# Making a weight tile's low part in two GpSimd instructions of half the width

## The chip, the cores and the metric

The kernel runs on one core of a Trainium2 chip. The metric is the device time of one execution in microseconds; the time before is the median of three runs. All that is read from inside an execution comes from one profiled run of the kernel.

## What is computed

One layer of a decoder trunk on 2048 positions of width 1024, all in float32:

```python
h = rmsnorm(x, norm_mix_w) * (1.0 + sc1) + sh1
proj = h @ w_in                      # 1024 x 3624
o_a = hgrn2_mixer(...)               # gated linear recurrence, 4 heads, chunkwise
o_b = dsa_mixer(...)                 # indexer, top 256 keys of each query, softmax over them
o_c = conv_module(...)               # GLU, causal depthwise conv (31 taps), LayerNorm, swish
x = x + g1 * (concat([o_a, o_b, o_c]) @ w_out)
h = rmsnorm(x, norm_mlp_w) * (1.0 + sc2) + sh2
x = x + g2 * (square(relu(h @ mlp_w1)) @ mlp_w2)      # 1024 -> 4096 -> 1024
return rmsnorm(x, final_norm_w)
```

The six vectors `sh1` ... `g2` come from `silu(c) @ ada_w + ada_b`.

## The kernel before

**Matrix products in three parts.** TensorE's fast float32 form drops low bits, so each operand is split into a high part (a copy rounded to that form) and a low part (the rest: source minus high part), and a product is three: high x high, high x low of the activation, low of the weight x high. The low part of the weight is used last of the three. A weight tile is 128 partitions x 1024 elements: 8 pieces of 128x128 or 4 of 128x256 (`mm_T`, L350; `n_part`, L1158).

**How a weight tile comes about.** `fetch_w` loads it into `wraw` (two buffers) by a DMA that SyncE issues; `split_w` takes a `whi` and a `wlo` (two buffers each) and calls `split`, where ScalarE casts the high part (L256) and GpSimd subtracts (L257). `split` has other callers, with tiles of 128x512 in two dimensions: the hidden activations of the MLP (`hl`) and the mixers' outputs (`ml`). `next_w` keeps one split tile and up to two loads ahead of the product that runs. The raw buffer is free for the next load when its low part is made, and SyncE's queue issues all loads in order.

**The stages.** The positions go in four blocks of 512. Block 0 of the input projection loads and splits `w_in`, and `keep_w` writes both parts to DRAM; blocks 1 to 3 load them ready made (tile `wk`), with no split. Beside it run the recurrence (`hgrn_gen`), the convolution (`conv_gen`), the indexer (`index_gen`), the key search (`topk_gen`) and attention (`attn_gen`) as generators that are stepped between products. Then come the output projection and the MLP, block by block; here every block loads and splits its weights anew, and the rest of indexer, search and attention runs beside it. Before the last block, `tsum_gen` adds quarters of MLP weights on VectorE and writes the sums to DRAM (`tsr`).

**The last block.** It goes through the MLP by a Strassen scheme: `produce` makes split tiles named X, Y, Z and W for each unit. X and Z are tiles of `swh`/`swl` (128 x 2 x 512), Y is `swy`, W is `sww` (a 128x512 tile in two dimensions). The string `LO_W` ("GVVG", or "GVGG" for odd units below 24) says which engine makes the low part (L1485): X and W are GpSimd's, Y is VectorE's, Z is VectorE's or, in the odd units, GpSimd's. The sums on activations (`s_parts`, L1359 to L1366) run on both engines. A product there uses one half of X, Y or Z, and the next product the other half.

**What sets the order.** The program is written as tiles and operations with a priority; when it is built, a planner walks it with a model of times, puts each engine's instructions in one fixed order, and sets the waits. On the chip each engine works through its order.

Of the kernel before, what the change touches and what calls it, by code (L numbers as in the profile page):

```python
# [8 lines left out]
F32 = mybir.dt.float32  # L9
# [7 lines left out]
OP = mybir.AluOpType  # L17
# [60 lines left out]
def trunk(ctx, tc, x, c, ada_w, ada_b, norm_mix_w, norm_mlp_w, w_in, hg_lb_logits,  # L78
# [3 lines left out]
    V, A, G, T = nc.vector, nc.scalar, nc.gpsimd, nc.tensor  # L82
# [18 lines left out]
    def nm(s):  # L101
        uid[0] += 1
        return f"{s}_{uid[0]}"
# [148 lines left out]
        rpow(rs, ss, 1, 1.0 / n)  # L252
        return rs

    def split(src, hi, lo, lo_eng=None):
        A.copy(hi, src)  # L256
        (lo_eng or G).tensor_tensor(lo, src, hi.bitcast(F32), OP.subtract)  # L257

    def to_act_steps(xh, acol, bcol, ah, al, mid=None):
        for k in range(NK):  # L260
# [37 lines left out]
    def split_w(raw, kk, m):  # L298
        hi = wp.tile([P, kk, m], F32R, tag="whi", bufs=WH, name=nm("whi"))
        lo = wp.tile([P, kk, m], F32R, tag="wlo", bufs=WL, name=nm("wlo"))  # L300
        split(raw, hi, lo)
        return hi, lo
# [812 lines left out]
    for pieces, ev, _ in in_units:  # L1115
        if ev in (ev_hi, ev_sv):
            o0, n, src = pieces[0]
# [52 lines left out]
    def mix_tiles(b, kh):  # L1170
        hh, hl = [], []
        for k in range(4):
            hi = mp.tile([P, TB], F32R, tag="hh", bufs=HB, name=nm("mh"))
            lo = mp.tile([P, TB], F32R, tag="hl", bufs=HB, name=nm("ml"))
            r = mp.tile([P, TB], F32, tag="hr", bufs=MR, name=nm("mr"))
            dma(r, mx_d[b][kh * 4 + k])
            split(r, hi, lo)
            hh.append(hi)
            hl.append(lo)
        return hh, hl  # L1180
# [141 lines left out]
    def eng(pat, i):  # L1322
        return G if pat[i] == "G" else V
# [94 lines left out]
    def strassen_prepare():  # L1418
# [4 lines left out]
        def fetch(u):  # L1423
            if u >= len(units) or u in raws:
                return
            what, g, i = units[u]
            r1 = wp.tile([P, 2, TB], F32, tag="wraw", bufs=WR, name=nm("wr1"))
            r2 = sx.tile([P, 4, TB], F32, tag="wr2", bufs=2, name=nm("wr2"))
            if u < NTS:
                quarter_dma(r1[:, 0], u, 0, 0)  # L1430
                dma(r1[:, 1], ts_d[u][:, 1])
                quarter_dma(r2[:, 2], u, 1, 1)
                dma(r2[:, 3], ts_d[u][:, 3])
                quarter_dma(r2[:, 0], u, 1, 0)
                dma(r2[:, 1], ts_d[u][:, 2])
            else:
                for dst, kh, nh in ((r1[:, 0], 0, 0), (r1[:, 1], 0, 1), (r2[:, 0], 1, 0), (r2[:, 2], 1, 1)):
                    quarter_dma(dst, u, kh, nh)
            raws[u] = r1, r2
# [3 lines left out]
        def t_sums(u):  # L1443
            r1, r2 = raws[u]
            t1 = xp.tile([P, TB], F32, tag="tf", bufs=2, name=nm("t1"))
            b11, b12, b21, t4, b22, t2 = r1[:, 0], r1[:, 1], r2[:, 0], r2[:, 1], r2[:, 2], r2[:, 3]
            pat = T_W if units[u][0] == "m1" else T_W2
            if u < NTS:
                dma(t1, ts_d[u][:, 0])
            else:  # L1450
                eng(pat, 0).tensor_tensor(t1, b12, b11, OP.subtract)
                eng(pat, 1).tensor_tensor(t2, b22, t1, OP.subtract)
                eng(pat, 2).tensor_tensor(b12, b22, b12, OP.subtract)
                eng(pat, 3).tensor_tensor(t4, b21, t2, OP.subtract)
            srcs[u] = {"X": r1, "Y": r2[:, 2:], "Z": r2[:, :2], "W": t1}
# [6 lines left out]
        def produce():  # L1462
            if not stream:
                return
            u, which = stream.pop(0)
            if which == "X" and u not in summed:
                fetch(u)
                t_sums(u)
                summed.add(u)
            if which == TSW and u + 1 < len(units):  # L1470
                fetch(u + 1)
                t_sums(u + 1)
                summed.add(u + 1)
            src = srcs[u][which]
            if which in "XZ":
                hi = wp.tile([P, 2, TB], F32R, tag="whi", bufs=WH, name=nm("swh"))
                lo = wp.tile([P, 2, TB], F32R, tag="wlo", bufs=WL, name=nm("swl"))
            elif which == "Y":
                hi, lo = [xp.tile([P, 2, TB], F32R, tag="xt", bufs=4, name=nm("swy")) for _ in range(2)]
            else:  # L1480
                hl = xp.tile([P, 2, TB], F32R, tag="xt", bufs=4, name=nm("sww"))
                hi, lo = hl[:, 0], hl[:, 1]
            A.copy(hi, src)
            lo_w = "GVGG" if u < NTS and u % 2 else LO_W
            eng(lo_w, "XYZW".index(which)).tensor_tensor(lo, src, hi.bitcast(F32), OP.subtract)  # L1485
            if which == "W":
                hi, lo = hl[:, 0:1], hl[:, 1:2]
            split_[u, which] = hi, lo
            if which == FEW:
                fetch(u + 2)  # L1490
# [3 lines left out]
        def early_start():  # L1494
            fetch(0)
            t_sums(0)
            summed.add(0)

        st3.update(units=units, produce=produce, split=split_, early=early_start)

    def strassen_block(b):
# [223 lines left out]
```

## Time and profile before

| | |
|---|---|
| median of 3 runs | 3166.78 us (3162.09 to 3168.3) |
| the profiled execution | 3161.17 us, of which the span of its instructions is 3159.5 us |
| granted TensorE clock, mean | 0.956 |
| busy: PE, DVE, ACT, POOL | 2859.4, 2085.6, 1537.0, 1715.5 us |
| weight tiles' low parts on GpSimd, 128x1024 | 257 of `wlo` (635.5 us), 42 of `swl` (109.5 us) |

PE is TensorE's matmuls, PEld its weight loads, DVE is VectorE, ACT ScalarE, POOL GpSimd, SP SyncE. Times of day within the span count from its first instruction. An engine's busy time includes time in which an instruction has started and is held up.

### The profile page before, as it was taken

The numbers are of one execution on the slowest core, as the hardware profiler recorded it, in microseconds if no ns is written. First come the engines' busy times: TensorE is split into PE (matmuls) and PEld (weight loads), VectorE is DVE, ScalarE is ACT, GpSimd is POOL, SyncE is SP. The second block draws the span as 40 slices with busy tenths as digits, with TensorE's granted clock in tenths as the row PEclk, the third lists the DMA queues.
The fourth block names the chain that finished last, engine by engine and source line by source line (L and its number), as shares of the span: only waits on it lengthen the run. The fifth ranks groups of instructions, "written<-read, shape, count | busy, mean of one in ns | idle before, by whom it ended". The sixth has DMA issues, their size and how long they took to land.

```text
span 3159.5 us, 50407 instructions
## 1 busy us (share of the span) xinstructions
PE 2859.4 (91%) x18352; PEld 2573.1 (81%) x18352; DVE 2085.6 (66%) x3673; ACT 1537.0 (49%) x2879; POOL 1715.5 (54%) x1231
## 2 busy tenths in 40 slices
PE   5979988898999989999999999998898898889987
PEld 4767868777787879888888889898787888889987
DVE  7785486867436444847776757576979631477787
ACT  3435444445313244555556556455544444456653
POOL 6555162225205255555767566576665656756675
PEclk9989999998999999999999999999999999999998
DMA  7856665564655343434546444455799953455533
GB/s 261 267 175 235 221 191 188 192 214 162 196 195 165 119 151 97 136 118 121 157 140 207 138 124 149 122 163 160 241 284 300 299 184 121 143 192 171 175 113 104
DMA packets 479413, 560.08 MB, mean 177 GB/s; under 512 B 32615, under 2 KB 371884, under 8 KB 479148
## 3 DMA queue, kind: packets, MB, share of 16 engines
q1 hardware_dynamic: 478992, 556.65, 55.9%
q8 instruction: 145, 2.38, 0.3%
q14 instruction: 120, 0.98, 0.1%
q10 hardware_dynamic: 156, 0.07, 0.0%
HBM read 458.30 MB, written 98.31 MB: 176 GB/s over the span
## 4 chain that ended last, share of the span: by engine, by line
PE 54%; DVE 22%; DMA 9%; issue 6%; ACT 4%; POOL 3%; SPq 1%; DVEq 0%; POOLq 0%; ACTq 0%
PE mm L350 18%; PE ax L1158 17%; PE mm L1158 5%; DVE cacc L523 2%; DMA adw<-in_ada_w_dram 2%; DVE s L752 2%; DVE cum L850 2%; DMA tsr<-in_mlp_w_dram 2%; PE po L932 1%; PE ix L745 1%; PE at L920 1%; SPq L106 1%; PE ax L632 1%; PE at L898 1%; DMA wr<-ts_d 1%
## 5 line engine op out<-in xcount | busy, mean ns | idle before, releaser
L257 POOL TENSOR_TENSOR wlo<-wraw,whi 128x1024 fp32r<-128x1024 f32 x257 | 635.5, 2473 | 479.6 <-ACT whi L256 343.0
L256 ACT CAST whi<-wraw 128x1024 fp32r<-128x1024 f32 x257 | 270.0, 1050 | 346.7 <-PE ax L1158 127.7
L752 DVE SCALAR_TENSOR_TENSOR s<-r,iw_s,s 128x512 f32<-128x512 f32 (+3 forms) x266 | 301.9, 1135 | 199.8 <-ACT r L747 197.1
L1158 PE MATMUL ax<-whi,hh 128*128 128x256 f32 x1600 | 282.9, 291 | 43.9 <-DVE acc L1302 32.8
L350 PE MATMUL mm<-ah,wk 128*128 128x512 f32 x1104 | 300.9, 405 | 8.1 <-issue 2.5
L1158 PE MATMUL ax<-whi,hl 128*128 128x256 f32 x1600 | 280.2, 289 | 2.2 <-POOL hl L257 2.2
L1158 PEld LDWEIGHTS ax<-whi,hh 128*128 128x128 f32 x1600 | 237.5, 195 | 54.4 <-DVE acc L1302 33.9
L350 PE MATMUL mm<-ah,whi 128*128 128x512 f32 x936 | 263.2, 406 | 16.3 <-DVE slo L463 9.3
L1158 PE MATMUL ax<-wlo,hh 128*128 128x256 f32 x1600 | 275.1, 287 | 0.0
L930 POOL TENSOR_TENSOR pT<-L,pT 128x512 fp32r<-128x512 f32 (+3 forms) x160 | 202.1, 1266 | 115.7 <-ACT pT L929 107.9
L350 PE MATMUL mm<-ah,wlo 128*128 128x512 f32 x936 | 255.4, 397 | 0.0
L350 PE MATMUL mm<-al,whi 128*128 128x512 f32 x936 | 254.9, 396 | 0.0
L350 PEld LDWEIGHTS mm<-ah,wk 128*128 128x128 f32 x1104 | 206.2, 193 | 51.3 <-issue 3.9
L747 ACT ACTIVATE r<-ix 128x512 f32<-128x512 f32 (+3 forms) x256 | 141.3, 552 | 216.3 <-PE ix L745 196.2
L1158 PEld LDWEIGHTS ax<-whi,hl 128*128 128x128 f32 x1600 | 235.0, 194 | 6.5 <-POOL hl L257 3.2
L1158 PEld LDWEIGHTS ax<-wlo,hh 128*128 128x128 f32 x1600 | 230.9, 193 | 2.2
L521 POOL TENSOR_TENSOR cside<-cside,ctap 128x512 f32<-128x512 f32 x112 | 165.3, 1476 | 120.9 <-ACT ctap L520 98.4
L350 PEld LDWEIGHTS mm<-ah,whi 128*128 128x128 f32 x936 | 177.0, 194 | 54.3 <-DVE slo L463 10.1
L350 PEld LDWEIGHTS mm<-ah,wlo 128*128 128x128 f32 x936 | 177.1, 191 | 37.0 <-POOL wlo L257 0.2
L350 PEld LDWEIGHTS mm<-al,whi 128*128 128x128 f32 x936 | 175.8, 190 | 35.8
L1302 DVE TENSOR_TENSOR acc<-acc,ax 128x512 f32<-128x512 f32 x160 | 109.1, 682 | 90.1 <-PE ax L1158 89.7
L850 DVE TENSOR_SCALAR_CACHE_REDUCE cum<-s,ssm 128x384 bf16<-128x384 f32 (+13 forms) x112 | 165.3, 1476 | 3.3 <-POOL s L756 1.4
(552 smaller groups left out, 6938.2 us busy)
## 6 DMA issues: line engine op xcount, KB each, us to landing
wraw<-in_mlp_w_dram SPq DMA_DIRECT2D x192, 512.0 KB
wk<-wk_d SPq DMA_DIRECT2D x174, 512.0 KB
kc<-sk_d SPq DMA_DIRECT2D x112, 256.0 KB
vc<-v_d SPq DMA_DIRECT2D x112, 256.0 KB
tsr<-in_mlp_w_dram SPq DMA_DIRECT2D x96, 256.0 KB
ts_d<-tsr SPq DMA_DIRECT2D x48, 512.0 KB
wr<-in_mlp_w_dram SPq DMA_DIRECT2D x96, 256.0 KB
wr<-ts_d SPq DMA_DIRECT2D x72, 256.0 KB
```

Source lines behind the costliest of these rows:

```text
L106: return nc.sync.dma_start(o, i)
L256: A.copy(hi, src)
L257: (lo_eng or G).tensor_tensor(lo, src, hi.bitcast(F32), OP.subtract)
L350: T.matmul(ps, ww[:, k, :], aa[k], start=(n == 0 and k0 == 0), stop=(n == len(order) - 1 and k1 == NK))
L521: G.tensor_tensor(side, side, tap, OP.add)
L523: V.scalar_tensor_tensor(acc, hc[:, w:w + TB], cvc[:, m, w:w + 1], acc, op0=OP.mult, op1=OP.add)
L747: A.activation(r[:, :w], ps[:, :w], AF.Relu, scale=32.0 ** -0.5)
L752: V.scalar_tensor_tensor(s[:, c0:c0 + w], r[:, :w], iw, s[:, c0:c0 + w], op0=OP.mult, op1=OP.add)
L850: V.tensor_scalar(dump, s, t, -AIM - i * STEP, op0=OP.is_ge, op1=OP.add, accum_out=d)
L930: G.tensor_tensor(pT[:, :nt, 1], lv, pT[:, :nt, 0].bitcast(F32), OP.subtract)
L1158: T.matmul(ps[:, t * 256:(t + 1) * 256], aa[f][:, tok * P:(tok + 1) * P], ww[:, f, :], start=(first and n == 0 and (last or t == 0)), stop ...
L1302: V.tensor_tensor(dst, dst, src, OP.add)
```

## The change

`split` loses its unused argument for another engine, and a new helper `low_part` makes the low part. Where the engine is GpSimd and the tile has three dimensions, it cuts the tile at half of its second dimension and issues two instructions, the first half first; else it issues one, as before. `split` and `produce` call it.

```diff
-    def split(src, hi, lo, lo_eng=None):
+    def split(src, hi, lo):
         A.copy(hi, src)
-        (lo_eng or G).tensor_tensor(lo, src, hi.bitcast(F32), OP.subtract)
+        low_part(G, lo, src, hi)
+
+    def low_part(e, lo, src, hi):
+
+        n = lo.shape[1]
+        cuts = (0, n // 2, n) if e is G and len(lo.shape) == 3 else (0, n)
+        for i, j in zip(cuts, cuts[1:]):
+            e.tensor_tensor(lo[:, i:j], src[:, i:j], hi[:, i:j].bitcast(F32), OP.subtract)
...
             A.copy(hi, src)
             lo_w = "GVGG" if u < NTS and u % 2 else LO_W
-            eng(lo_w, "XYZW".index(which)).tensor_tensor(lo, src, hi.bitcast(F32), OP.subtract)
+            low_part(eng(lo_w, "XYZW".index(which)), lo, src, hi)
```

ScalarE's cast of the high part, the loads, the buffers and the matmuls are as before.

## Rows read from the trace of the kernel before

**Rows 1.** The page: its first line, part 1 (busy us, share of the span, instructions) and the shares of the chain that ended last, by engine.

```profile
span 3159.5 us, 50407 instructions
PE 2859.4 (91%) x18352; PEld 2573.1 (81%) x18352; DVE 2085.6 (66%) x3673; ACT 1537.0 (49%) x2879; POOL 1715.5 (54%) x1231
...
PE 54%; DVE 22%; DMA 9%; issue 6%; ACT 4%; POOL 3%; SPq 1%; DVEq 0%; POOLq 0%; ACTq 0%
```

**Rows 2.** Busy time of the engines in stretches of the span. Columns: from and to, length, then PE, PEld, DVE, ACT and POOL busy us (instructions), granted clock, DMA share, GB/s.

```profile
0.00:320.00 320.00, 255.70 (x1362) 216.59 (x1363) 236.91 (x465) 145.61 (x259) 183.65 (x146) 0.92 0.71 233
...
1195.00:2200.00 1005.00, 955.60 (x6235) 870.50 (x6234) 669.86 (x1213) 553.11 (x997) 633.28 (x432) 0.98 0.46 139
2200.00:2540.00 340.00, 300.79 (x1862) 267.86 (x1861) 281.07 (x388) 165.09 (x300) 206.41 (x123) 0.95 0.90 278
...
2768.00:3110.00 342.00, 311.07 (x2488) 304.78 (x2487) 269.79 (x304) 199.80 (x329) 230.77 (x132) 0.98 0.48 154
```

**Rows 3.** The same, of the instructions that write or read the tile `wlo` alone; columns PE, PEld and POOL busy us (instructions), then clock and DMA.

```profile
0.00:320.00 320.00, 70.47 (x280) 50.26 (x280) 72.43 (x29) 0.92 0.71 233
320.00:950.00 630.00, 0.00 (x0) 0.00 (x0) 0.00 (x0) 0.94 0.61 196
...
1195.00:2200.00 1005.00, 339.38 (x1721) 267.06 (x1720) 335.08 (x137) 0.98 0.46 139
2200.00:2540.00 340.00, 104.32 (x508) 81.26 (x508) 109.30 (x43) 0.95 0.90 278
```

**Rows 4.** Groups of POOL's instructions by line and shape, whole span: line, engine, operation, out<-in, shapes, count, then busy us, mean ns of one, and idle time before them with its releasers.

```profile
L257 POOL TENSOR_TENSOR wlo<-wraw,whi 128x1024 fp32r<-128x1024 f32 x257 | 635.5, 2473 | 479.6 <-ACT whi L256 343.0 <-PE mm L350 40.9 <-DMA wraw<-in_w_out_dram 17.7
...
L257 POOL TENSOR_TENSOR hl<-hr,hh 128x512 fp32r<-128x512 f32 x96 | 139.5, 1454 | 23.0 <-ACT hh L256 22.9
L1485 POOL TENSOR_TENSOR swl<-wr,swh 128x1024 fp32r<-128x1024 f32 x42 | 109.5, 2608 | 78.9 <-ACT swh L1483 75.2 <-DMA t<-ts_d 2.5 <-DMA wr<-ts_d 1.1
```

**Rows 5.** The page's part 5, the weight loads of TensorE that read `wlo`: busy us, mean ns, and after the second bar the idle time before them and its releaser.

```profile
L1158 PEld LDWEIGHTS ax<-wlo,hh 128*128 128x128 f32 x1600 | 230.9, 193 | 2.2
...
L350 PEld LDWEIGHTS mm<-ah,wlo 128*128 128x128 f32 x936 | 177.1, 191 | 37.0 <-POOL wlo L257 0.2
```

**Rows 6.** POOL's instructions in order of time, 1401.5 to 1411 us: start us, duration us, engine, line, operation, out<-in, shapes; in brackets idle time before and what ended it.

```profile
1402.18 2.40 POOL L257 TENSOR_TENSOR wlo<-wraw,whi 128x1024 fp32r<-128x1024 f32 x1 [1.88 <-ACT whi L256]
1404.54 1.33 POOL L257 TENSOR_TENSOR hl<-hr,hh 128x512 fp32r<-128x512 f32 x1
...
1408.46 2.40 POOL L257 TENSOR_TENSOR wlo<-wraw,whi 128x1024 fp32r<-128x1024 f32 x1 [0.35 <-PE ix L745]
```

**Rows 7.** The same view, 2933 to 2944 us, in the last block.

```profile
2934.71 1.30 POOL L1549 TENSOR_TENSOR hl<-r,hh 128x512 fp32r<-128x512 f32 x1
2935.96 2.28 POOL L1485 TENSOR_TENSOR sww<-t,sww 128x512 fp32r<-128x512 f32 x1
2939.78 3.08 POOL L1485 TENSOR_TENSOR swl<-wr,swh 128x1024 fp32r<-128x1024 f32 x1 [1.54 <-ACT swh L1483]
```

**Rows 8.** The chain of work that ended last, in the last block (2768 to 3110 us): shares of this stretch by line, as far as the line goes.

```profile
by line: issue 10.3%; POOL swl L1485 7.7%; DMA wr<-ts_d 7.5%; DMA wr<-in_mlp_w_dram 5.4%; DVE swl L1485 4.9%; PE ax L1534 4.7%; PE at L1534 4.7%; PE mm L1523 4.7%; PE mm L1534 4.6%; DVE sr L1362 4.5%; DVE acc L1588 4.3%; PE at L1523 4.1%; P
```

**Rows 9.** Waits of SyncE's DMA queue, whole span: line, what it waited for, us in total, times, longest us.

```profile
SPq L106 <- POOL wlo L257: 506.6, 161, 11.9
...
SPq L106 <- POOL swl L1485: 107.5, 34, 7.9
```

**Rows 10.** DVE's instructions in order of time, from 1404 to 1412 us and from 2938 to 2945 us (columns as in group 6).

```profile
1409.07 1.95 DVE L752 SCALAR_TENSOR_TENSOR s<-r,iw_s,s 128x128 f32<-128x128 f32 x1 [4.34 <-ACT r L747]
...
1411.90 0.41 DVE L752 SCALAR_TENSOR_TENSOR s<-r,iw_s,s 128x128 f32<-128x128 f32 x1 [0.28 <-ACT r L747]
...
2940.51 2.62 DVE L1362 TENSOR_TENSOR sr<-r,sr 128x256 f32<-128x256 f32 x1
```

**Rows 11.** Three lines of the code, their instructions over the span: count, then least, median and longest ns, first and last start us, shapes. L752 and L1362 take both tensors from SBUF, L1302 takes one from PSUM.

```profile
L752 DVE SCALAR_TENSOR_TENSOR s<-r,iw_s,s x266: 333/752/2922, 99.6 to 2391.5; 128x512 f32<-128x512 f32 x100, 128x384 f32<-128x384 f32 x14, 128x128 f32<-128x128 f32 x10, 128x256 f32<-128x256 f32 x9
...
L1302 DVE TENSOR_TENSOR acc<-acc,ax x160: 659/683/689, 1246.4 to 2648.5; 128x512 f32<-128x512 f32 x160
...
L1362 DVE TENSOR_TENSOR sr<-r,sr x14: 412/1366/2624, 2802.5 to 3076.0; 128x256 f32<-128x256 f32 x14
```

**Rows 12.** Groups of DVE's instructions by line and shape, from 1195 to 2540 us (columns as in group 4). Of the four `tsr` lines (L1400, L1401, L1403, L1404, 24 instructions each) the one with the longest and the one with the shortest mean stand here.

```profile
L752 DVE SCALAR_TENSOR_TENSOR s<-r,iw_s,s 128x512 f32<-128x512 f32 x173 | 220.6, 1275 | 117.5 <-ACT r L747 116.2
L1302 DVE TENSOR_TENSOR acc<-acc,ax 128x512 f32<-128x512 f32 x142 | 96.7, 681 | 54.7 <-PE ax L1158 54.2
...
L1401 DVE TENSOR_TENSOR tsr<-tsr,tsr 128x512 f32<-128x512 f32 x24 | 33.0, 1375 | 11.5 <-DMA tsr<-in_mlp_w_dram 11.4
...
L1400 DVE TENSOR_TENSOR tsr<-tsr 128x512 f32<-128x512 f32 x24 | 25.9, 1081 | 9.0 <-DMA tsr<-in_mlp_w_dram 8.8
```

**Rows 13.** Waits of PE from 1195 to 2540 us: what it waited for, us in total, times, longest us.

```profile
PE ax L1158 <- DVE acc L1302: 32.8, 10, 11.5
...
PE mm L265 <- DVE ah L274: 8.5, 1, 8.5
```

**Rows 14.** Pieces of the chain in order of time, 2930 to 2945 us: start us, us, engine and line.

```profile
2930.94 2.43 POOL swl L1485
...
2933.39 3.60 DMA wr<-in_mlp_w_dram
```

## The prediction

> **What bounds the kernel now.** I read the page's parts 1 and 4 first [rows 1]: TensorE is busy for 2859.4 of 3159.5 us, and the chain that ended last lies on PE for 54% of the span, on DVE for 22% and on POOL for 3%. TensorE is the bound, and what can be won is its 300 us of idle time. Then I read the stretches [rows 2]: between 1195 and 2200 us PE idles for 49 of 1005 us, between 2200 and 2540 for 39 of 340, in the last block (2768 to 3110) for 31 of 342. The first 320 us have 64 us of idle, with VectorE busy for 237 of them. The same windows for the tile `wlo` alone [rows 3] say where the change acts: 29 instructions in the first 320 us, none from there to 950 us (the weights come back ready made), 137 between 1195 and 2200, 43 up to 2540. The last block has its own 42, of the tile `swl` [rows 4]. In all 257 + 42 = 299 instructions of 128x1024 become 598 of 128x512. The low parts of activations (`hl`, `ml`, `al`) and `sww` have two dimensions, and those that VectorE makes are not GpSimd's: they stay whole.
>
> **Does PE wait for these tiles?** Hardly. The two groups of weight loads that read `wlo` show 0.2 us of waiting for it in the first and none in the second [rows 5]. In nearly every product the low part is used last, behind two thirds of the product. So the first half, ready some 1.1 us earlier, is worth 0.2 us at most: I take 0. The matmuls that read the second half get a wait for POOL of their own; as the tile is long done when they come, I cost it at 0; if that cover went, each tile would cost PE at most the 1.1 us by which the second half follows the first.
>
> **The price on GpSimd.** Start to start, a 128x1024 instruction that is followed at once takes 1404.54 - 1402.18 = 2.36 us [rows 6] and a 128x512 one 2935.96 - 2934.71 = 1.25 us [rows 7]. A pair takes 2.50 us, 0.14 us more; 299 pairs make 42 us on an engine that is busy for 1715 of 3159 us. That alone is covered nearly everywhere by POOL's idle 46%. Where it is not covered is the chain: POOL's 3% is 95 us, of which `swl` has 7.7% of 342 us = 26 us in the last block [rows 8], about 11 tiles. Of the other 69 us I give `wlo` its share of POOL's remaining busy time, 635 of 1606 us: 27 us, another 11 tiles (an estimate). 22 tiles at 0.14 us are +3 us. The upper end is for a VectorE instruction that slips in between the halves: 0.41 to 0.75 us more for each, 0.9 us in all, +20 us. Most tiles on the path will not meet one, so I take +4.
>
> SyncE stands behind this: it issues the loads in order, and waits for `wlo` 161 times, 506.6 us, and for `swl` 34 times, 107.5 us [rows 9], as the raw tile is free only when its low part is made. What is queued behind such a load (keys and values of attention, the next sums) is 0.14 us later for each tile. On POOL itself `hl` and the attention's `pT` are queued behind the pair. Both are within the terms above, as the chain passes through them.
>
> **The gain on VectorE.** This is what the change can win. A VectorE instruction that takes two operands from SBUF does not run beside a GpSimd instruction: it stands until that one has ended. L752 on 128x128 started at 1409.07 and took 1.95 us, while `wlo` ran from 1408.46 to 1410.86 [rows 6, 10]; at 1411.90 the same instruction took 0.41. Over the span L752 has a median of 0.75 and a longest of 2.92 us, while L1302, which has one operand in PSUM, never exceeds 0.689 us [rows 11]. The Trainium skill, page SBUF — State Buffer, section "Who interferes with whom", says that the pair of ports that the two engines share is held for a whole instruction by whoever starts first, and that the other is fully blocked; these rows agree. With halves the longest stand behind one instruction falls from 2.4 to 1.3 us.
>
> Between 1195 and 2540 us [rows 12]: L752 of 128x512, 173 x (1.275 - 0.75) = 91 us; the four `tsr` lines, 96 instructions at the mean of the first and the last, 1.23 us, against 0.68 for an undisturbed add (L1302): 53 us. Of these 144 us, wide tiles hold 444 of POOL's 840 busy us [rows 2, 3], and who meets one waits up to 2.4 us, not 1.3: 444 x 2.4 / (444 x 2.4 + 396 x 1.3) = 67%, 97 us. Halves cut it to half if nothing else comes in between: -48 us; but VectorE's next instruction then meets the second half, so I take half of that, -24 us. DVE has 22% of the chain: -5.3 us at the end. Bounds: 0, and -20, half of the 41 us (32.8 + 8.5) that PE waits for DVE in these rows [rows 13]. For the 73 wide tiles before 1195 and between 2540 and 2768 (257 less these 180 and the last 4) I take the same per tile: -2.1 us. In the last block L1362 has a least of 0.412 and a median of 1.366 us, 14 times [rows 11], and 4.5% of the block's chain [rows 8]: at 2940.51 it stood for 2.62 us behind `swl`, 3.08 us long here [rows 7, 10]. A release 1.1 us earlier is worth 15 us if every one meets a first half and nothing else is late; half of them, and PE already busy for 91% of the block: -4 us.
>
> **Sum.** -5.3 - 2.1 - 4 + 4 = -7.4 us. The profiled execution took 3161.2 us (span 3159.5), 5.6 us under the median of 3166.8. On its own time the sum gives 3153.8, on the median 3159.4. I forecast **3159 us**; where a stand goes, what is late next is PE's own work.
>
> **Rivals.** (1) The stands shrink and nothing comes of it: PE is 95% busy between 1195 and 2200 us, and the waits that it has for DVE are ends of long queues. For it speaks that the wide tile is not once a named releaser of PE worth over 0.2 us; against it the 22% of DVE on the chain. 3166 us, give or take 5. (2) Slower: GpSimd's pair ends late. VectorE takes the ports at the gap, the second half stands behind it, and the raw tile, SyncE's queue and the next load are late by 0.9 us and not 0.14. At 22 tiles that is 20 us, with 7 to 8 of the gain kept on the other side: +12, 3179 us. It decides where the next load is what the stage waits for, as in the last block, whose chain runs from `swl` (2.43 us) straight into a load (3.60 us) [rows 14]. The Trainium skill has the rule that would do this on the same page and section: issue order, not the shape of an operation, decides who blocks; by it every gap with a waiting VectorE instruction is lost to GpSimd. No row of before can show it, since there is no gap in the middle of a tile. (3) The order on the engines moves. The program's order is planned when it is built, from readiness; with a tile ready in two steps another matmul or add may be put first. The longest single wait of PE for a DVE add is 11.5 us [rows 13]: one such wait more or less, 3155 or 3178. (4) The split does not do what it says (readers still wait for the whole tile): the VectorE part stays, so this is within (1).
>
> **How the numbers follow.** Forecast 0.45, its own range -20 to -1 us, 3147 to 3166; (1) 0.27; (2) 0.20; (3) 0.08. A measurement of this kernel can tell 0.2%, 6.3 us, from no change. Faster by more: 0.33 of the forecast's, 0.04 of (3), 0.02 of (1): 0.39. Within: 0.12 + 0.20 + 0.02 = 0.34. Slower: 0.18 of (2), 0.04 of (3), 0.05 of (1): 0.27. The range takes the larger part of the forecast's own and reaches to (2) and (3): 3143 to 3181.
>
> **What would show it.** Right: L752's mean at 128x512 between 1195 and 2540 us falls from 1.28 toward 1.1 us and the longest stands to about 2 us where two meet; POOL's busy time grows by 40 to 100 us; PE's waits for DVE between 1195 and 2540 us shrink by a few us; `wlo` pairs lie 1.25 us apart. Wrong: pairs that are over 3 us long as a rule, SyncE's wait for `wlo` above 560 us, and a chain with more POOL than 3%: then (2). If DVE's busy time falls by 40 us or more and PE's idle time stays 300 us: (1). If PE's idle time moves in stretches without wide tiles (320 to 950 us): (3).

## The result and the profile after

The changed kernel takes 3064.37 us (median of 5 runs, 3060.93 to 3070.88) against 3166.78 us (5 runs, 3162.09 to 3168.99): ratio 0.9682, 95% interval 0.9667 to 0.9698. That is 102 us less. The forecast was 7 us less and its range ended at 3143: the sign was right, the size was not, by far. The lines below `split` are numbered 7 higher than before (L752 is L759, L1302 is L1309, L1158 is L1165), and all of GpSimd's low parts that `split` and `produce` make are now L264. Kernels cut after planning keep the numbers of the plan's source.

The page of the changed kernel, first line and part 1 (before: [rows 1]):

```profile
span 3063.2 us, 50800 instructions
...
PE 2831.0 (92%) x18352; PEld 2554.6 (83%) x18352; DVE 1982.8 (65%) x3673; ACT 1541.4 (50%) x2883; POOL 1792.8 (59%) x1530
```

The span is 96.3 us shorter. VectorE's busy time fell by 102.8 us with the same 3673 instructions, GpSimd's grew by 77.3. PE's idle time went from 300 to 232 us (3063.2 - 2831.0), and its busy time fell by 28 with the same instructions. The granted TensorE clock rose from 0.956 to 0.966, and busy time times clock is the same in both (2734 and 2735 us; 2728 to 2744 in all 20 traces of this case). So 68 of the 96 us are idle time and 28 are the same work at a higher clock; why the clock was higher is not shown. The chain that ended last breaks off early in this trace (its shares sum to 69%), so I don't set it beside that of before.

GpSimd's wide tiles and VectorE's lines in the changed kernel, whole span for `wlo` and `swl` (before: [rows 4]), 1156 to 2467 us for the rest, which is the stretch of [rows 12]:

```profile
L264 POOL TENSOR_TENSOR wlo<-wraw,whi 128x512 fp32r<-128x512 f32 x514 | 719.3, 1420 | 406.8 <-ACT whi L256 269.6 <-PE mm L357 32.9 <-DMA wk_d<-wlo 23.7
...
L264 POOL TENSOR_TENSOR swl<-wr,swh 128x512 fp32r<-128x512 f32 x84 | 122.0, 1477 | 63.7 <-ACT swh L1490 55.7 <-PE ax L1541 3.1 <-PE at L1541 2.5
...
L759 DVE SCALAR_TENSOR_TENSOR s<-r,iw_s,s 128x512 f32<-128x512 f32 x174 | 188.0, 1081 | 138.2 <-ACT r L754 137.6
```

The mean of L752 at 128x512 went from 1275 to 1081 ns, as foreseen. Its longest over the span, and the lines for comparison (count, then least, median and longest ns; before: [rows 11]):

```profile
L759 DVE SCALAR_TENSOR_TENSOR s<-r,iw_s,s x266: 335/784/1897, 98.9 to 2316.3; 128x512 f32<-128x512 f32 x100, 128x384 f32<-128x384 f32 x14, 128x128 f32<-128x128 f32 x10, 128x256 f32<-128x256 f32 x9
...
L1309 DVE TENSOR_TENSOR acc<-acc,ax x160: 655/686/690, 1207.8 to 2571.6; 128x512 f32<-128x512 f32 x160
```

The longest of these instructions now takes 1.90 and not 2.92 us, and the add with one operand in PSUM is where it was. The rule that the prediction took from the Trainium skill, page SBUF — State Buffer, section "Who interferes with whom" (the pair of ports is held for a whole instruction), agrees with this: a shorter GpSimd instruction goes with a shorter stand.

Now where the 96 us came from. I cut the span at five marks that both traces have: first and last matmul that reads `wk`, first add of L1302, first `tsr`, first matmul with `swl`. Busy time by stretch (columns as in [rows 2]), before:

```profile
0.00:309.70 309.70, 245.40 (x1306) 207.71 (x1307) 230.67 (x456) 136.50 (x236) 177.70 (x134) 0.92 0.72 234
309.70:1070.40 760.70, 691.34 (x4047) 593.23 (x4046) 475.18 (x1086) 311.59 (x701) 235.01 (x238) 0.95 0.58 189
...
1246.40:2244.00 997.60, 945.02 (x6128) 858.10 (x6128) 699.46 (x1252) 551.59 (x1001) 638.33 (x436) 0.98 0.48 145
...
2774.60:3159.50 384.90, 339.13 (x2706) 332.43 (x2704) 296.22 (x339) 212.68 (x364) 242.79 (x141) 0.96 0.46 148
```

and after:

```profile
0.00:297.40 297.40, 243.38 (x1307) 206.48 (x1307) 222.47 (x456) 136.52 (x236) 185.29 (x163) 0.94 0.75 243
297.40:1037.50 740.10, 685.63 (x4047) 586.87 (x4046) 473.08 (x1086) 316.10 (x705) 230.56 (x238) 0.96 0.61 195
...
1207.80:2176.80 969.00, 936.27 (x6130) 853.10 (x6130) 646.90 (x1253) 552.37 (x1001) 675.21 (x569) 0.99 0.49 150
...
2697.10:3063.20 366.10, 333.18 (x2705) 326.85 (x2703) 282.31 (x339) 211.28 (x364) 256.01 (x186) 0.98 0.48 156
```

The second line of each is the one to look at. Between the first and the last `wk` matmul GpSimd has the same 238 instructions, there is hardly a wide tile to cut, VectorE's busy time is within 2 us, and yet the stretch is 20.6 us shorter. The prediction named just this as the mark of rival (3): the order on the engines has moved. What PE waited for there, before:

```profile
PE ax L654 <- DVE k L598: 12.8, 4, 6.9
PE ax L632 <- DVE k L598: 10.0, 5, 4.0
PE ax L640 <- DVE k L598: 8.4, 5, 4.9
PE at L944 <- POOL ot L942: 4.9, 1, 4.9
```

and after:

```profile
PE ax L647 <- DVE k L605: 15.9, 5, 4.6
PE at L905 <- DVE mx L907: 5.0, 1, 5.0
PE ax L639 <- DVE k L605: 3.5, 4, 1.3
PE ax L661 <- DVE k L605: 3.5, 2, 2.9
```

The recurrence's three waits for `k` are in both lists, 31.2 us before and 22.9 after, but shared out otherwise (one is twice as long as before, two are a third), and most of the smaller waits are others. The order of the instructions in the two traces says why. PE and VectorE have the same instructions in both, but taken by operation, names and shapes 13% of PE's and 24% of VectorE's are out of line with the order of before (longest common order: 15889 of 18352 and 2783 of 3673).

So there are two theories. **Stands**: VectorE stands for a shorter time behind GpSimd, as predicted, only with a larger effect. **Order**: the planner, given tiles that are ready in two steps, puts another order on the engines, and this is what pays.

### The profile page after: what moved, and what is told of

The parts are those of the page before. It is cut to its first block, busy times and chain, and to the rows that moved or that the text cites. A ratio compares the mean times of both kernels' runs of the same rounds, so it can differ in the third digit from the quotient of the medians.

```text
span 3063.2 us, 50800 instructions
## 1 busy us (share of the span) xinstructions
PE 2831.0 (92%) x18352; PEld 2554.6 (83%) x18352; DVE 1982.8 (65%) x3673; ACT 1541.4 (50%) x2883; POOL 1792.8 (59%) x1530
## 4 chain that ended last, share of the span: by engine, by line
PE 47%; DVE 8%; DMA 4%; issue 4%; POOL 3%; ACT 2%; SPq 1%; DVEq 0%; POOLq 0%; ACTq 0%
PE ax L1165 18%; PE mm L357 14%; PE ix L752 1%; PE po L939 1%; PE at L905 1%; PE at L927 1%; DMA tsr<-in_mlp_w_dram 1%; PE mm L1165 1%; PE at L1165 1%; POOL wlo L264 1%; PE ax L1530 1%; PE at L1541 1%; PE ax L1541 1%; SPq L106 1%; PE at L1530 1%
## 5 line engine op out<-in xcount | busy, mean ns | idle before, releaser
L264 POOL TENSOR_TENSOR wlo<-wraw,whi 128x512 fp32r<-128x512 f32 x514 | 719.3, 1420 | 406.8 <-ACT whi L256 269.6
L759 DVE SCALAR_TENSOR_TENSOR s<-r,iw_s,s 128x512 f32<-128x512 f32 (+3 forms) x266 | 261.9, 984 | 209.7 <-ACT r L754 208.5
L1165 PE MATMUL ax<-whi,hh 128*128 128x256 f32 x1600 | 282.5, 290 | 30.4 <-DVE acc L1309 20.7
L1165 PE MATMUL ax<-whi,hl 128*128 128x256 f32 x1600 | 280.5, 288 | 2.4 <-POOL hl L264 2.4
L1165 PE MATMUL ax<-wlo,hh 128*128 128x256 f32 x1600 | 274.0, 287 | 0.0
L1165 PEld LDWEIGHTS ax<-whi,hh 128*128 128x128 f32 x1600 | 235.8, 193 | 39.8 <-DVE acc L1309 19.6
L357 PE MATMUL mm<-ah,whi 128*128 128x512 f32 x936 | 255.7, 399 | 10.3 <-DVE slo L470 3.0
L1165 PEld LDWEIGHTS ax<-whi,hl 128*128 128x128 f32 x1600 | 233.5, 193 | 5.6 <-POOL hl L264 3.2
L1165 PEld LDWEIGHTS ax<-wlo,hh 128*128 128x128 f32 x1600 | 231.2, 193 | 2.6
L1309 DVE TENSOR_TENSOR acc<-acc,ax 128x512 f32<-128x512 f32 x160 | 109.1, 682 | 96.4 <-PE ax L1165 96.1
```

Source lines behind the costliest of these rows:

```text
L264: e.tensor_tensor(lo[:, i:j], src[:, i:j], hi[:, i:j].bitcast(F32), OP.subtract)
L357: T.matmul(ps, ww[:, k, :], aa[k], start=(n == 0 and k0 == 0), stop=(n == len(order) - 1 and k1 == NK))
L759: V.scalar_tensor_tensor(s[:, c0:c0 + w], r[:, :w], iw, s[:, c0:c0 + w], op0=OP.mult, op1=OP.add)
L1165: T.matmul(ps[:, t * 256:(t + 1) * 256], aa[f][:, tok * P:(tok + 1) * P], ww[:, f, :], start=(first and n == 0 and (last or t == 0)), stop ...
L1309: V.tensor_tensor(dst, dst, src, OP.add)
```

## Experiments

Each kernel is compared with before on its own chip. A ratio below 1 is faster, and one point of it (0.01) is 31.7 us. "Plan" is what the planner was given when it set the order; "chip" is how the low parts are cut in the instructions that run.

**The two halves of the change alone.** In the first kernel the planner sees whole tiles, so the order of every engine is that of before, and each of the 299 wide instructions is replaced by two halves afterwards, in place:

```diff
     with tile.TileContext(nc, schedule_with_timeline_sim=True) as tc:
         trunk(tc, *args, o)
+    halve(nc)
... (in halve, for each of the 299 instructions)
+            ins[k] = i.__replace__(name=nc.get_next_instruction_name(), outs=tuple(_cut(p, 0, 512) for p in i.outs),
+                                   ins=tuple(_cut(p, 0, 512) for p in i.ins),
+                                   sync_info=i.sync_info.__replace__(on_update=()))
+            ins.insert(k + 1, i.__replace__(outs=tuple(_cut(p, 512, 1024) for p in i.outs),
+                                            ins=tuple(_cut(p, 512, 1024) for p in i.ins),
+                                            sync_info=i.sync_info.__replace__(on_wait=())))
```

> The plan is that of the kernel before, instruction for instruction on every engine; after planning, each of the 299 wide low parts is replaced by its two halves, the first with the waits, the second with the signal. Theory A (the 102 us come from the order in which the planner put the engines' work once it saw two instructions): little is left, 3155 to 3172 us. Theory B (they come from GpSimd holding the ports for a shorter time): most of the gain is here, 3065 to 3090 us.

The second has the order of the changed kernel, and the first half is then widened to 1023 columns and the second narrowed to the last one, so that all but one column is one instruction again:

```diff
         trunk(tc, *args, o)
+    whole(nc)
...
+                ins[k] = i.__replace__(outs=tuple(_wide(p, 1023) for p in i.outs), ins=tuple(_wide(p, 1023) for p in i.ins))
...
+                ins[k] = i.__replace__(outs=tuple(_cut(p, 511, 512) for p in i.outs),
+                                       ins=tuple(_cut(p, 511, 512) for p in i.ins))
```

> The plan is that of the changed kernel; after planning, the first half is widened to 1023 of 1024 columns and the second cut to the last column, so GpSimd works in one wide instruction and a short one behind it. Theory A (order): the gain stays, 3065 to 3090 us, dearer by some of the short instructions. Theory B (shorter holds of the ports): the gain is gone, 3155 to 3190 us. If both take part, between.

Measured: halves in the old order 3118.63 us, ratio 0.9841 (0.9825 to 0.9858); the new order with long instructions 3091.24, 0.9756 (0.9739 to 0.9772). Either alone is faster than before, and neither reaches the 0.9682 of both. The first lies between the ranges of its two theories, the second next to that of theory A: both theories take part. Part 1 of the page, halves in the old order:

```profile
PE 2850.3 (91%) x18352; PEld 2567.8 (82%) x18352; DVE 1991.1 (64%) x3673; ACT 1536.2 (49%) x2879; POOL 1794.1 (57%) x1530
```

and long instructions in the new order:

```profile
PE 2839.6 (92%) x18352; PEld 2561.0 (83%) x18352; DVE 2046.4 (66%) x3673; ACT 1541.3 (50%) x2883; POOL 1790.6 (58%) x1530
```

In the old order VectorE loses 94.5 us of busy time and the end moves by 36 us in the profiled execution and by 49 in the median: the stands are real and worth 1.59 points. In that run the order of all instructions on PE, VectorE and ScalarE is that of before, to the last one, so the cut on GpSimd is all that differs. In the new order VectorE keeps the larger part of its stands (2046.4, of the 102.8 us 39 stay away; its L759 goes up to 2.95 us again), and the end moves by more. Stretch by stretch, lengths in us from the same view and marks:

| | to first `wk` | to last `wk` | to L1302 | to `tsr` | to `swl` | to the end | span |
|---|---|---|---|---|---|---|---|
| before | 309.7 | 760.7 | 176.0 | 997.6 | 530.6 | 384.9 | 3159.5 |
| old order, halves | 307.2 | 759.3 | 172.8 | 985.3 | 525.7 | 373.3 | 3123.6 |
| new order, long | 301.3 | 740.9 | 169.3 | 976.1 | 529.3 | 377.0 | 3093.9 |
| after | 297.4 | 740.1 | 170.3 | 969.0 | 520.3 | 366.1 | 3063.2 |

The halves alone gain where wide tiles are (-12 in the long stretch, -5, -12 in the last block) and 1 us where there are none. The 20 us of the second column belong to the order, whichever way the tiles are cut on the chip.

**How far does an order move by itself?** Two kernels change nothing of the work: before, with one of the planner's rates (how fast it lets the side work of block 1 or 2 go) changed by about 1%.

```diff
-R1 = [1126, 1216, 1594]
+R1 = [1136, 1216, 1594]
```

> The kernel before with one step rate of the planner's background work (the indexer) at 1136 for 1126: a control for how much the order alone moves the time, with whole tiles. Theory A (order): the time may move by tens of us either way, 3100 to 3240 us. Theory B (ports): within 0.5% of before, 3150 to 3183 us.

> The kernel before with the rate of the key search at 1230 for 1216: a second control of the order alone. Theory A: 3100 to 3240 us. Theory B: 3150 to 3183 us.

(The second has 1230 in place of 1216.) Measured: 3141.98 us, 0.9921 (0.9904 to 0.9937), and 3145.93, 0.9922 (0.9905 to 0.9938). Whole tiles in another order are 25 us faster than before, as theory A had it (3100 to 3240 us) and not theory B (within 0.5%). So an order is a draw of some size, and before has a slower one than these two. One new order that gains 77 us proves little about halves in the plan until several are seen.

**Which tiles make the order?** Halves for the 29 tiles of `w_in` alone, and for the other 270 alone:

```diff
-            ready.append((f, sp) if sp is None else (split_w(*f), sp))
+            ready.append((f, sp) if sp is None else (split_w(*f, two=sp[1] == "win"), sp))
... (the argument is handed on to low_part; the other kernel has != in place of ==)
```

> Halves, planned and run, for the 29 tiles of the input projection alone (0 to 320 us); all other low parts whole. Theory A1 (what the order gained before 1100 us, some 33 us, is set by these 29 tiles): 3115 to 3145 us, with a gain that grows in the stretch from 320 to 950 us where no low part is made. Theory A2 (the order's gain belongs to the order as a whole, a draw among many): anywhere in 3090 to 3170 us. If block 0 had no part in it: 3160 to 3170 us.

> Halves for all but those 29 tiles. The plan is the same as before up to about 1000 us, so nothing can be won earlier but by chance. Theory A1: the shorter holds give 40 to 47 us, and the order after 1000 us some 20 to 45 more: 3080 to 3110 us. Theory A2: the order after 1000 us is a new draw, 3080 to 3150 us.

Measured: 3112.93 us, 0.9835 (0.9808 to 0.9863), and 3109.27, 0.982 (0.9798 to 0.9841); in us -52 and -56. That they add up to about the 102 of both says little, as the three kernels run three different orders in the last two thirds. Neither result tells theory A1 from A2: the first is just under A1's range and in A2's, the second in both. The first is the plainest single result for the order. Part 1 of its page:

```profile
PE 2845.6 (91%) x18352; PEld 2562.6 (82%) x18352; DVE 2084.0 (67%) x3673; ACT 1539.5 (49%) x2883; POOL 1725.4 (55%) x1260
```

VectorE is as busy as before (2084.0 against 2085.6), so little or nothing is won from the stands, and the kernel is 52 us faster with 29 tiles cut in the first 300 us. Its trace has the order of the changed kernel until after the last `wk` matmul, which comes 26 us earlier than before (1044.4 against 1070.4); the other 26 us come later, where its tiles are whole and its order is a new one. The second kernel has the order of before until after that matmul and has gained nothing there (1071.0).

**The change with the other rates**, and the four combinations of plan and chip for each:

> The changed kernel with the indexer's rate at 1136, to be compared with the kernel before at that rate (3142 us). Theory A1 (the planner gains as a rule from a tile in two steps): 65 to 110 us less than its own whole version, 3032 to 3077 us. Theory A2 (one lucky order): the shorter holds alone, 27 to 50 us less, and an order that is drawn anew, 3080 to 3130 us.

> The changed kernel with the key search's rate at 1230, to be compared with the kernel before at that rate (3146 us). Theory A1: 3036 to 3081 us. Theory A2: 3085 to 3135 us.

> At the indexer's rate of 1136: the plan with whole tiles (3142 us as planned), halves put in after planning. The shorter holds alone, in another order than before. If they are worth 27 to 50 us whatever the order: 3092 to 3115 us. If the 49 us of the first such run belonged to that order: 3120 to 3142 us.

> At the same rate: the plan with halves, on the chip 1023 columns and 1. Theory S (a plan made with halves is better as a rule): 3092 to 3130 us. Theory D (a draw): 3130 to 3160 us.

> At the key search's rate of 1230: the plan with whole tiles (3146 us as planned), halves put in after planning. Shorter holds worth 27 to 50 us: 3096 to 3119 us; if they belong to one order: 3125 to 3146 us.

> At the same rate: the plan with halves, on the chip 1023 columns and 1. Theory S: 3090 to 3120 us. Theory D: anywhere in 3095 to 3160 us, so that only a value above 3125 would speak against S.

And a third rate (1610 in place of 1594), planned and run whole, and planned and run in halves:

> The kernel before with the third rate (attention) at 1610 for 1594: one more order with whole tiles, to be the partner of the next run. From the three orders so far (3142 to 3168 us): 3130 to 3180 us.

> The changed kernel at the same rate. Theory S (holds and plan, as a rule): 55 to 105 us below the run before it, 3040 to 3100 us. Theory D (holds alone, the order drawn anew): 20 to 55 us below it.

Measured, ratios with their 95% intervals (us in the same order: e7 3086.34, e8 3065.96, f1 3099.82, f2 3118.87, f3 3096.36, f4 3092.35, f5 3125.09, f6 3078.44):

| rates | plan whole, chip whole | plan whole, chip halves | plan halves, chip 1023+1 | plan halves, chip halves |
|---|---|---|---|---|
| as in before | 1 | 0.9841 (0.9825-0.9858) | 0.9756 (0.9739-0.9772) | 0.9682 (0.9667-0.9698) |
| 1136 | 0.9921 (0.9904-0.9937) | 0.9787 (0.9767-0.9807) | 0.9858 (0.9837-0.9878) | 0.9760 (0.9741-0.9778) |
| 1230 | 0.9922 (0.9905-0.9938) | 0.9785 (0.9767-0.9804) | 0.9768 (0.9742-0.9794) | 0.9686 (0.9667-0.9704) |
| 1610 | 0.9880 (0.9854-0.9905) | | | 0.9732 (0.9708-0.9756) |

Not every cell of the last two columns is an order of its own. With halves in the plan, the traces at 1230 and at the rates of before have the same order on PE, VectorE, ScalarE and GpSimd, to the last instruction (by operation, names and shapes). So 0.9682 and 0.9686 are one order measured twice, as are 0.9756 and 0.9768, and there are four orders planned with whole tiles but three with halves. The forecasts went both ways: the halves in place kept theirs for shorter holds (3099.82 and 3096.36 us); of the new orders, that at 1136 fell in theory S's range with long instructions and in A2's with halves, and that at 1610, 47 us below its partner, in D's.

Second column less first: the stands alone, with no engine's order moved, are worth 1.59, 1.34 and 1.37 points (each to about 0.25). They hardly depend on the order: 42 to 50 us, mean 45. VectorE's busy time falls with them from 2092.7 to 1996.4 and from 2095.4 to 1994.8 us under the two other rates.

Fourth less second: planning with halves is worth 1.59, 0.27 and 0.99 points (each to about 0.27). The first and the third set one new order against two old ones, and the second is no larger than its interval. Fourth less first: the whole change is worth 3.18, 1.61, 2.36 and 1.48 points. The mean of the four whole orders is 0.9931, of the three with halves 0.9725: some 2.05 points, 65 us, are what the change does on the mean of the orders seen. Of these the stands are 1.43 (45 us; not measured at 1610), which leaves 0.6 (20 us) for the plan. The other 1.1 points (36 us) of the measured 3.18 are which orders were met: before lies 0.69 above its column's mean, the slowest of four, and after 0.43 below its own, the fastest of three.

The third column is not the plan alone. VectorE is busy in it for 2046.4, 2053.6 and 2047.2 us, 39 to 48 us less than with whole tiles at the same rate, though the long instructions are as long as before. So it holds part of the stands' gain, and it gains more over the first column (2.44, 0.63 and 1.54 points) than the plan adds to halves. Why VectorE stands less there is not shown, and the two parts do not simply add up.

**Is the plan's part a rule or luck?** Against the scatter at the end three new orders are few. Earlier in the span more can be seen. The matmuls that read `wk`, first and last start, in six kernels (plan whole and chip halves, then after, then whole and halves under the third rate, then two of the next experiment: second half first, and 1023 columns and 1 in plan and chip):

```profile
L350 PE MATMUL mm<-ah,wk x1104: 387/390/796, 307.2 to 1066.5; 128*128 128x512 f32 x184
```

```profile
L357 PE MATMUL mm<-ah,wk x1104: 387/389/797, 297.4 to 1037.5; 128*128 128x512 f32 x184
```

```profile
L350 PE MATMUL mm<-ah,wk x1104: 387/389/796, 308.0 to 1054.0; 128*128 128x512 f32 x184
```

```profile
L357 PE MATMUL mm<-ah,wk x1104: 387/389/796, 296.8 to 1042.9; 128*128 128x512 f32 x184
```

```profile
L357 PE MATMUL mm<-ah,wk x1104: 386/390/882, 298.4 to 1056.1; 128*128 128x512 f32 x184
```

```profile
L360 PE MATMUL mm<-ah,wk x1104: 387/389/796, 302.3 to 1067.5; 128*128 128x512 f32 x184
```

Under the four rates the first start is 309.7, 310.4, 308.6 and 308.0 us with whole tiles in plan and chip, and 297.4, 298.0, 296.3 and 296.8 with halves in both: 12 us, without overlap. With halves on the chip alone it is 307.2, 309.1 and 305.7, so some 10 of the 12 are the plan's. But these are not four draws each: up to that matmul the traces show one order of PE's instructions under three of the four rates with whole tiles (1136 has another), and one under all four with halves (at 1136 up to 287 us). What speaks for a rule is that three further new orders start early too: second half first at 298.4 us, 1023 columns and 1 in the plan at 302.3, quarters (below) at 286.0. Against it, the halves' order run with 1023 columns and 1 starts at 301.3, 297.7 and, at 1136, 308.4 us.

At the last start the means are 1066 and 1044 (the four: 1070.4, 1068.9, 1072.3, 1054.0 against 1037.5, 1054.3, 1040.2, 1042.9), and 1068 with halves on the chip alone; here the two groups touch. So some 10 us in block 0 look like a rule for tiles that are planned in more than one instruction. What comes behind, up or down, goes with the order that was met. At the end, all orders planned and run with all 299 tiles in halves or finer (0.9682 to 0.9779, those of the next experiments included) lie below the three that were planned whole and cut in place (0.9785 to 0.9841). That too speaks for a rule, but the two groups all but touch.

**What in two-step readiness does it?** Two kernels ask. In one the second half is made first, so that each half is ready when the other would be. In the other the planner itself is given 1023 columns and one column: two instructions, hardly two steps.

```diff
-        for i, j in zip(cuts, cuts[1:]):
+        for i, j in reversed(list(zip(cuts, cuts[1:]))):
```

```diff
-        n = lo.shape[1]
-        cuts = (0, n // 2, n) if e is G and len(lo.shape) == 3 else (0, n)
+        if e is G and len(lo.shape) == 3:
+            lo, src, hi = [t.rearrange("p k m -> p (k m)") for t in (lo, src, hi)]
+            cuts = (0, 1023, 1024)
+        else:
+            cuts = (0, lo.shape[1])
```

> The changed kernel with the second half made first: GpSimd's work is the same, but the half that the products read first is the later one, in the plan and on the chip. Theory P1 (the planner gains since products may start on a tile that is half done): the order's part is lost, 3105 to 3140 us. Theory P2 (it gains whatever half is first; readiness of the first half is not the cause): 3055 to 3090 us.

> Planned and run as 1023 columns and 1 column: on the chip GpSimd does what it did in the run with the new order and whole tiles (3091 us), but the planner sees this split and not halves. Theory P1 (half a tile ready early): the order's gain is gone, 3140 to 3185 us. Theory P2 (a second instruction and more planned GpSimd time are what moves the order): 3075 to 3110 us.

Measured: 3094.89 us, 0.9779 (0.9759 to 0.9799), and 3136.64, 0.9901 (0.9882 to 0.9921). The first is 31 us slower than after and lies between the ranges of both theories. The second has the same kinds of instructions on the chip as the third column of the table (0.9756, 0.9858 and 0.9768), and it is slower than each of these, as P1 said, though 3 us below P1's range. So at the end both point to an early first half. Block 0 points the other way: both kernels start on `wk` early (298.4 and 302.3 us, against 297.4 for halves and 301.3 for the halves' order with long instructions), so the gain there needs neither the first half first nor a half at all. What they lose they lose behind it, from the first to the last `wk` matmul (757.7 and 765.2 us, against 740.1 in after), where no such tile is made. As orders alone differ by 1.2 points (the first column), that can be the order met, and neither run settles it.

**Finer, and more of it.** Quarters of 128x256, and halves for GpSimd's low parts in two dimensions too (`hl`, `ml`, `sww`):

```diff
-        n = lo.shape[1]
-        cuts = (0, n // 2, n) if e is G and len(lo.shape) == 3 else (0, n)
+        if e is G and len(lo.shape) == 3:
+            lo, src, hi = [t.rearrange("p k m -> p (k m)") for t in (lo, src, hi)]
+            cuts = (0, 256, 512, 768, 1024)
+        else:
+            cuts = (0, lo.shape[1])
```

```diff
-        cuts = (0, n // 2, n) if e is G and len(lo.shape) == 3 else (0, n)
+        cuts = (0, n // 2, n) if e is G else (0, n)
```

> Four instructions of 128x256 in place of two of 128x512. If the shorter hold is what counts, VectorE stands less again, by half of what the halves won at most (10 to 25 us at the end), against some 80 us more work on GpSimd: 3040 to 3075 us. If GpSimd's work and the late end of the tile count more: 3075 to 3110 us.

> Halves for the low parts in two dimensions too (the MLP's hidden values, the mixers' outputs, the tile W of the last block: 128x512 into two of 128x256). If short holds pay wherever VectorE runs beside: 3035 to 3062 us. If those tiles are waited for by the products (they are, by some us) and their later end costs as much: 3062 to 3090 us.

Measured: 3075.49 us, 0.9705 (0.9684 to 0.9726), and 3067.41, 0.9684 (0.9666 to 0.9702): no better than halves, at and within the slower of the two ranges each. Part 1 and the tile's group, with quarters:

```profile
PE 2836.6 (92%) x18352; PEld 2557.9 (83%) x18352; DVE 1926.6 (63%) x3673; ACT 1542.4 (50%) x2883; POOL 1900.4 (62%) x2128
...
L267 POOL TENSOR_TENSOR wlo<-wraw,whi 128x256 fp32r<-128x256 f32 x1028 | 828.2, 836 | 376.7 <-ACT whi L256 266.7 <-PE mm L360 37.8 <-issue 18.4
```

VectorE gains another 56 us of busy time, GpSimd works 108 longer, and the end is no earlier. Each of the two kernels is again another order, and orders with halves alone differ by 0.8 points. So what finer cuts would bring in one and the same order is not shown.

## Why the prediction was wrong, step by step

**What can be won is PE's 300 us of idle time: not all of it.** Of the 96 us, 28 came from PE's busy time, which the prediction took as fixed; it fell as the granted clock rose (above).

**PE does not wait for these tiles: right.** PE's waits for `wlo` stay under 1 us in total in the old order with halves and are not in the list of after. The weight loads that had 0.2 us before [rows 5], in the old order with halves:

```profile
L350 PEld LDWEIGHTS mm<-ah,wlo 128*128 128x128 f32 x936 | 175.8, 189 | 36.7 <-POOL wlo L257 0.6
```

**The gain on VectorE: right mechanism, mis-sized twice.** The step read "Halves cut it to half if nothing else comes in between: -48 us; but VectorE's next instruction then meets the second half, so I take half of that, -24 us. DVE has 22% of the chain: -5.3 us at the end." The same lines in the old order with halves, 1188 to 2515 us (before: [rows 12]):

```profile
L752 DVE SCALAR_TENSOR_TENSOR s<-r,iw_s,s 128x512 f32<-128x512 f32 x173 | 188.7, 1091 | 132.7 <-ACT r L747 131.4
L1302 DVE TENSOR_TENSOR acc<-acc,ax 128x512 f32<-128x512 f32 x142 | 96.7, 681 | 66.0 <-PE ax L1158 65.6
L1401 DVE TENSOR_TENSOR tsr<-tsr,tsr 128x512 f32<-128x512 f32 x24 | 27.3, 1138 | 14.5 <-DMA tsr<-in_mlp_w_dram 14.3
...
L1400 DVE TENSOR_TENSOR tsr<-tsr 128x512 f32<-128x512 f32 x24 | 24.7, 1027 | 10.9 <-DMA tsr<-in_mlp_w_dram 10.8
```

L752 gave 220.6 - 188.7 = 31.9 us and the four `tsr` lines about 13: 45 us, nearly the 48 that I had before I halved it, and not 24. So the second meeting that I feared took little here. Then these were not all the lines that stand: of the 94.5 us over the span half is elsewhere, for instance the 16 of L1212 (1482 to 1036 ns) and the 96 of L598 (634 to 551 ns). L1212 reads only one full tensor (its other operand is a column), so not only the lines with two tensors in SBUF stand, as I had it. My terms came to some 42 us of VectorE's time in all (24, 2.1 / 0.22 = 10, and 14 x 1.1 / 2 = 8). And the weight was wrong: 94.5 us of VectorE moved the end by 49 (36 by the profiled execution), 0.4 to 0.5 of it and not 0.22; under the other two rates 96.3 and 100.6 us moved the end by 42 and 43. The chain's share is a mean over all of VectorE's work; in these runs the time that it stands was worth more than that mean. Why is not tested here. I had -11.4 us for these terms and +4 for GpSimd's price, -7.4 together; together they measured -42 to -50.

**The price on GpSimd: right in kind, a little low.** What it costs at the end is within the -42 to -50 us. The pair took 716.5 / 257 = 2.79 us with halves in the old order against 2.473: +0.32 and not +0.14, as VectorE does slip in. GpSimd's busy time grew by 78.6 us there (foreseen: 40 to 100).

**Rival (2), VectorE takes the ports at the gap: seen, but it does not decide.** Two pairs of the old order with halves, one alone and one that is met; GpSimd's timeline:

```profile
1388.25 2.55 POOL L257 TENSOR_TENSOR wlo<-wraw,whi 128x512 fp32r<-128x512 f32 x2 [1.62 <-ACT whi L256]
...
1586.08 3.80 POOL L257 TENSOR_TENSOR wlo<-wraw,whi 128x512 fp32r<-128x512 f32 x2 [1.37 <-ACT whi L256]
```

and VectorE's at the second:

```profile
1587.18 1.54 DVE L812 SCALAR_TENSOR_TENSOR s<-cum,s 128x1280 f32<-128x1280 bf16 x1 [0.99 <-DVE far L864]
```

L812 comes 1.1 us after the pair began, goes at the gap and ends at 1588.72; the second half ends at 1589.88, and the pair takes 3.80 in place of 2.55 us. This row agrees with the rule of the Trainium skill, page SBUF — State Buffer, section "Who interferes with whom", that issue order decides who blocks. But pairs of over 3 us are not the rule: between 1300 and 2300 us 22 of 136 rows with the tile show it. SyncE's waits (before: [rows 9]):

```profile
SPq L106 <- POOL wlo L257: 516.2, 165, 9.4
...
SPq L106 <- POOL swl L1485: 114.7, 36, 8.4
```

Up by 10 and 7 us, well under the 560 that I had set as the mark of rival (2). In after they are 426.5 and 76.4. The one mark of it that did come, GpSimd with 4% and not 3% of the chain in the old order with halves, cost less than VectorE gained, as the end came 49 us earlier.

**Rival (3), the order moves: a right cause, left out of the sum and priced at one wait.** This is the step that failed most: about half of the 102 us are the order. The sum has no term for it. I gave it a chance of 0.08 and +-11.5 us, since "The longest single wait of PE for a DVE add is 11.5 us". A new plan does not move one wait: some 13% of PE's instructions changed place, and many waits of a few us with them. Orders of the same work scatter over 3125 to 3168 us with whole tiles, and planning with halves gained 9 to 50 us more (0.27 to 1.59 points, where all of it runs in halves). The long waits tell it too, PE's for the add in the changed kernel, whole span (before: [rows 13]):

```profile
PE ax L1165 <- DVE acc L1309: 20.7, 7, 5.5
```

The longest is now 5.5 us; in the old order with halves the 11.5 us are still there (27.2 us in 8). The whole row fell from 32.8 to 20.7 us, 12 of the 96.

The forecast mechanism, shorter stands, accounts for 42 to 50 of the 102 us, so its sign would have been right without a new order. The other half is no part of the forecast, and some 36 us of it are the luck of the two orders met.

**What stays open.** How much of the plan's part is a rule: the 20 us rest on four orders with whole tiles and three with halves, and the ends scatter by 1.2 and 0.8 points. Why an order planned with cut tiles is better in block 0 was only narrowed: the cut of the 29 tiles of `w_in` alone brings it, it comes with the second half first and with 1023 columns and 1 too, and no single wait carries it. Why the granted clock rises as the kernel gets faster is not shown.

## What to carry to other kernels

Where a planner sets the order, a small edit has two effects: price the edit in the order that is there, and separately allow for a new order, by the scatter that a neutral edit (here a rate moved by 1%) shows, not by one wait. Cutting in place after planning shows the first effect by itself, in one run. Before orders are counted as separate draws, compare them in the traces: a moved rate can leave the order as it was. When an engine stands behind another's long instruction, count all lines whose longest time is far over their median; here 0.4 to 0.5 of the time saved reached the end, twice the engine's share of the chain.

## What the runs showed of the hardware

- A subtraction of 1023 columns on GpSimd takes 2476 ns on the mean and one of a single column still 438 ns, times in which they are held up included (257 of each, in the new order with long instructions): a very narrow instruction is not free.
- Quarters take 836 ns on the mean against 1420 for halves, so four cost 3.34 us, two 2.84, one whole 2.47: each further cut costs GpSimd 0.25 to 0.4 us, VectorE's slipping in included.
- With halves in place VectorE's busy time shrank by nearly the same 94.5, 96.3 and 100.6 us under three different orders.
- TensorE's busy time and its granted clock went together: 2859.4 us at 0.956 before, 2831.0 at 0.966 after, the product 2728 to 2744 in all 20 traces.
